# SwiGLU's activation turned by transposing transfers in place of TensorE

## The chip, the cores and the metric

The kernel runs on one core of one Trainium2 chip. The metric is device time of one execution in microseconds (us). Engines are named as in the profile: PE is TensorE's matmul side and PEld its weight loads, DVE is VectorE, ACT is ScalarE, POOL is GpSimd, SP is SyncE, which issues most DMA transfers. Each engine works through its own list of instructions in order.

## The reference

One layer of a decoder on 256 tokens of width 2048, in float32: an attention branch and a recurrent branch are merged, then comes the feed-forward network, then a gated embedding. The change lies in the feed-forward network alone:

```python
h = rms_norm(x, g_ffn_pre[layer])
gate, up = jnp.split(h @ w_gate_up[layer], 2, axis=-1)
x = x + rms_norm((jax.nn.silu(gate) * up) @ w_down[layer], g_ffn_post[layer])
```

`w_gate_up` is 2048 x 11264 and `w_down` is 5632 x 2048.

## The kernel before

**Tiles.** P is 128 and NB is 512. The 256 tokens are two chunks c of 128. The hidden width of 5632 is 11 blocks j of 512 columns (NJ). A product is made in three matmuls: every float32 operand is split into a rounded high part and the rest (`hi`/`lo` for activations, `wh`/`wl` for weights), and hi·wh, lo·wh and hi·wl are summed in a PSUM bank (`terms`, L473). Some groups of four weight tiles (quads) are done with seven products instead of eight (`by_quads`, L520).

**Preparing weights.** SP loads a pair of 128 x 512 weight tiles (`raw`, 512 KB) into one of six buffers; ACT makes `wh`, DVE makes `wl`, and for the quads DVE also makes sums `t` that ACT and DVE split in turn (`parts_of_pair`, L342; `parts_of_quad`, L364). Up to 61 general slots of 128 x 512 words (`slot`, L236) and seven `wh`/`wl` buffers hold what PE has not used yet.

**What sets the order.** The program is written by generators. A planner's clock advances with each matmul (0.227 us for a wide one, L40). A side task is a generator that yields what it waits for: an engine (its planned end), a tile, or a number of microseconds; `pump` (L219) continues those that are due. So side work is put among the matmuls at build time, and each engine then works in that fixed order.

**SwiGLU.** For block j, PE makes the gate and up products for both chunks. At the block's end DVE sums the partial results (`total`, L585), ACT applies Silu to the gate (`ev_g`, L1624), DVE multiplies (`ev_u`, L1638). The result t, 128 tokens x 512 columns, must be turned so that `w_down`'s products find the hidden width on the partitions. `gated` (L1609) does this: `transpose4` (L656) waits until three of the eight PSUM banks are free (`misc`, L270), has PE transpose four 128 x 128 squares against an identity into one bank, ACT copies the bank to `actT`, SP stores `actT` to a DRAM tile `actd[c][j]`. That is 22 tiles, two per block, and 88 transposes. From block 10 on POOL loads them back as `act` (`act_parts`, L1671) for the down product.

Because `misc` asks for three free banks, the transposes of most blocks stand one block late in the order: those of block 1 come when block 2's sums have been taken out.

Of the kernel before, what the change touches and what calls it, by code (L numbers as in the profile page):

```python
# [13 lines left out]
F32 = mybir.dt.float32  # L14
F32R = mybir.dt.float32r
I32 = mybir.dt.int32
AF = mybir.ActivationFunctionType
ALU = mybir.AluOpType
AX = mybir.AxisListType

P = 128
D = 2048
NB = 512
# [6 lines left out]

TABLES = (AF.Sigmoid, AF.Silu, AF.Exp, AF.Ln, AF.Sin)
TABLE_LOAD = 1.3
# [96 lines left out]
def block_kernel(ctx: ExitStack, tc: tile.TileContext, I, out: bass.AP):  # L129
# [24 lines left out]
    class InOrder:  # L154
# [20 lines left out]
        def __getattr__(self, name):  # L175
            f = getattr(self.engine, name)

            def call(o, *a, **kw):
                if name != "dma_start":
                    self.estimate(name, o, a, kw)  # L180
                return tc.keep_in_program_order(f(o, *a, **kw))  # L181

            return call

    V = InOrder(nc.vector, 0.07, 0.00105)
    A = InOrder(nc.scalar, 0.16, 0.0008)
    G, T, S = InOrder(nc.gpsimd, 0.9, 0.002), InOrder(nc.tensor, 0.0, 0.0), InOrder(nc.sync, 0.0, 0.0)
# [9 lines left out]
    def transpose(o, i, idn):  # L197
        clock[0] += SMALL
        T.transpose(o, i, idn)
# [29 lines left out]
    def nm(s):  # L229
        count[0] += 1  # L230
        return f"{s}_{count[0]}"
# [4 lines left out]
    def slot(s, shape=(P, NB), dt=F32):  # L236
        i = free_slots.popleft()
        t = slots.tile(list(shape), dt, tag=f"s{i}", name=nm(s))
        owner[id(t)] = i, t
        return t  # L240

    def free(*tiles):
        for t in tiles:
            free_slots.append(owner.pop(id(t))[0])
# [18 lines left out]
    def drop(ps):  # L263
        banks.append(bank_of.pop(id(ps))[0])
# [5 lines left out]
    def misc():  # L270
        while len(banks) < 3:
            yield 0.3
        return bank("misc")

    def act(o, i, f, **kw):
        return A.activation(o, i, f, **kw)

    def tt(o, a, b, op):
        return V.tensor_tensor(o, a, b, op)
# [12 lines left out]
    def cols(h, d=P):  # L292
        return slice(h * d, (h + 1) * d)
# [21 lines left out]
    def split_pair():  # L315
# [3 lines left out]
        if isinstance(raw, list):  # L319
            parts = [(slot("wh", dt=F32R), slot("wl", dt=F32R)) for j in range(2)]  # L320
            for (hi, lo), r in zip(parts, raw):
                act(hi, r, AF.Copy)
                tt(lo, r, hi.bitcast(F32), ALU.subtract)
            done = partial(free, *parts[0], *parts[1])
            free(*raw)
        elif len(in_pool) < SPLIT + 1:
            hi = wsplit.tile([P, 2, NB], F32R, tag="wh", name=nm("wh"))
            lo = wsplit.tile([P, 2, NB], F32R, tag="wl", name=nm("wl"))
            act(hi, raw, AF.Copy)
            tt(lo, raw, hi.bitcast(F32), ALU.subtract)  # L330
            parts, done = [(hi[:, j, :], lo[:, j, :]) for j in range(2)], in_pool.popleft
            in_pool.append(k)
        else:
            parts = [(slot("wh", dt=F32R), slot("wl", dt=F32R)) for j in range(2)]
            for j in range(2):
                act(parts[j][0], raw[:, j, :], AF.Copy)
            for j in range(2):
# [4 lines left out]
    def parts_of_pair():  # L342

        w, k, col, raw, _ = loaded.popleft()
        if len(in_pool) <= SPLIT:
            hi = wsplit.tile([P, 2, NB], F32R, tag="wh", name=nm("wh"))
            lo = wsplit.tile([P, 2, NB], F32R, tag="wl", name=nm("wl"))
            in_pool.append(k)
            act(hi, raw, AF.Copy)
            yield  # L350
            tt(lo, raw, hi.bitcast(F32), ALU.subtract)
            parts, done = [(hi[:, j, :], lo[:, j, :]) for j in range(2)], in_pool.popleft
        else:
            parts = [(slot("wh", dt=F32R), slot("wl", dt=F32R)) for j in range(2)]
            for j in range(2):
                act(parts[j][0], raw[:, j, :], AF.Copy)
            yield
# [271 lines left out]
    def lookup(groups):  # L629
        def there(g):  # L630
            return g in groups if isinstance(groups, dict) else len(groups) > g and groups[g] is not None

        def f(k):
            hurry(lambda: there(k // 4))
            hi, lo = groups[k // 4]
            return hi[:, k % 4, :], lo[:, k % 4, :]
        f.groups = groups
        return f
# [17 lines left out]
    def transpose4(src):  # L656
        ps = yield from misc()
        for i in range(4):
            transpose(ps[:, cols(i)], src[:, cols(i)], ident)
        return ps  # L660
# [146 lines left out]
    sinks = amask[:, 256:272]  # L807
    posi = cst.tile([P, 2], I32, name="posi")

# [223 lines left out]
    def hgrn_core(c, g):  # L1033
# [55 lines left out]
        def scores(lev):  # L1089
# [22 lines left out]
            if lev < 5:  # L1112
                V.copy_predicated(
                    right(sc),
                    cmask[:, cols(lev, 64)].rearrange("p (n w) -> p n w", w=w).unsqueeze(1)
                    .broadcast_to([P, 4, nb, w]).bitcast(I32),
                    pv.rearrange("p h (n w) -> p h n w", w=w))
# [488 lines left out]
    stored, parts, sides, down_sides = [set(), set()], [], {}, {}  # L1606
    h2T = [lookup(n.groups) for n in norm2]

    def gated(c, j, t):  # L1609

        pa = yield from transpose4(t)
        free(t)
        yield T
        at = slot("actT")
        act(at, pa, AF.Copy)
        drop(pa)
        S.dma_start(actd[c][j], at)
        free(at)
        stored[c].add(j)

    def swiglu(j):
# [16 lines left out]
        def ev_u(c, ps):  # L1638
            def f():
                if j in BY_QUADS and SEVEN:  # L1640
                    t = yield from total(us, 1, c, ps)
                    while sg[c] is None:
                        yield 0.3
                    yield sg[c]
                    stt(t, t, norm2[c].r, sg[c], ALU.mult, ALU.mult)
                    free(sg[c])
                else:
                    while sg[c] is None:
                        yield 0.3
                    t = sg[c]  # L1650
                    stt(t, ps, norm2[c].r, t, ALU.mult, ALU.mult)
                    drop(ps)
                yield V
                yield from gated(c, j, t)
            chain(f())
# [199 lines left out]
```

## Time and profile before

| | |
|---|---|
| Times of three runs | 1487.32, 1487.96 (median), 1491.14 us |
| The profiled execution's own time | 1489.56 us |
| Its span, first to last instruction | 1487.5 us |
| Mean granted TensorE clock | 0.997 |
| Gate and up products of blocks 0 to 10 | about 690 to 1155 us of the span |
| HBM read, written | 298.08 MB, 15.21 MB |

Busy time is a union over an engine's instructions. PE's matmuls overlap: one lasts 0.39 us, and the next one starts 0.227 us after it. What a group of PE instructions costs is therefore read from starts in the timeline and not from durations. DVE's and ACT's instructions overlap by some 0.1 us.

### The profile page before, as it was taken

To read this page: it belongs to the slowest core of one execution; us is meant where nothing else is said; L and a number is where in the kernel's file an instruction comes from. 1 tells how busy PE (TensorE), PEld (TensorE's weight loads), DVE (VectorE), ACT (ScalarE), POOL (GpSimd) and SP (SyncE) were. 2 spreads that over 40 slices of the span, in tenths; PEclk is the share of its full clock that TensorE was granted. 3 is DMA by queue.
4 is the path that set the end of the run, shared out by engine and by line. 5 is a ranking of instruction groups with operands and counts; after the bars stand their busy time and mean duration, and the time that the engine had idled before them with its cause. 6 is when DMAs were issued, how large, how long until landed. Compare 5 with 4: busy or idle time off the path is not lost.

```text
span 1487.5 us, 19958 instructions
## 1 busy us (share of the span) xinstructions
PE 1469.5 (99%) x6838; PEld 1216.3 (82%) x6838; DVE 1239.9 (83%) x2043; ACT 888.9 (60%) x1417; POOL 62.9 (4%) x107
## 2 busy tenths in 40 slices
PE   9999999999999999999999999999999999999997
PEld 6888888888887888888888888888888887888885
DVE  6878958755999867977899999999988899997773
ACT  7755655566666645665655666565655666575661
POOL 2100000000000100000000000000000000010000
PEclk9999999999999999999999999999999999999998
DMA  9754544345576856866756676576677678797551
GB/s 342 257 188 155 171 141 128 114 128 170 184 240 227 309 185 201 272 227 199 252 182 219 205 238 213 174 230 206 215 239 268 214 252 270 214 336 260 192 188 56
DMA packets 159557, 314.59 MB, mean 211 GB/s; under 512 B 11072, under 2 KB 11520, under 8 KB 159456
## 3 DMA queue, kind: packets, MB, share of 16 engines
q1 hardware_dynamic: 153024, 293.38, 61.0%
q0 software_dynamic: 6256, 19.88, 3.7%
q8 instruction: 53, 0.87, 0.2%
q14 instruction: 48, 0.39, 0.1%
q10 hardware_dynamic: 176, 0.07, 0.0%
HBM read 298.08 MB, written 15.21 MB: 211 GB/s over the span
## 4 chain that ended last, share of the span: by engine, by line
PE 64%; DVE 4%; issue 2%; DMA 1%; ACT 1%; DVEq 0%; POOLq 0%; POOL 0%; ACTq 0%
PE acc L181 63%; DVE wl L181 2%; PE misc L181 1%; DVE u L181 1%; ACT wh L181 1%; DVE t L181 1%; DMA raw<-in_w_in 1%; DMA raw<-in_w_down 0%; DMA raw<-in_w_gate_up 0%; DVE eg L181 0%; DVE slo L181 0%; DVE lo L181 0%; ACT hi L181 0%; DVE sides L181 0%; DVE s L181 0%
## 5 line engine op out<-in xcount | busy, mean ns | idle before, releaser
L181 PE MATMUL acc<-wh,hi 128*128 128x512 f32 x1769 | 700.2, 396 | 3.6 <-DVE u L181 2.4
L181 DVE TENSOR_TENSOR wl<-raw,wh 128x1024 fp32r<-128x1024 f32 (+1 forms) x606 | 595.7, 1007 | 115.4 <-ACT wh L181 113.8
L181 PE MATMUL acc<-wl,hi 128*128 128x512 f32 x1769 | 690.0, 390 | 0.0
L181 PE MATMUL acc<-wh,lo 128*128 128x512 f32 x1769 | 688.9, 389 | 0.0
L181 ACT ACTIVATE wh<-raw 128x1024 fp32r<-128x1024 f32 (+1 forms) x606 | 514.3, 883 | 239.8 <-PE acc L181 101.6
L181 PEld LDWEIGHTS acc<-wl,hi 128*128 128x128 f32 x1769 | 332.0, 188 | 71.2 <-DVE wl L181 1.1
L181 PEld LDWEIGHTS acc<-wh,hi 128*128 128x128 f32 x1769 | 332.3, 188 | 70.6 <-DVE u L181 3.2
L181 PEld LDWEIGHTS acc<-wh,lo 128*128 128x128 f32 x1769 | 332.5, 188 | 66.6 <-issue 0.2
L181 ACT ACTIVATE wh<-t 128x512 fp32r<-128x512 f32 x236 | 145.6, 628 | 106.6 <-DVE t L181 85.9
L181 DVE TENSOR_TENSOR wl<-t,wh 128x512 fp32r<-128x512 f32 x236 | 152.2, 683 | 0.5 <-PE acc L181 0.5
L181 DVE TENSOR_TENSOR u<-acc,u 128x512 f32<-128x512 f32 x132 | 86.3, 684 | 18.8 <-PE acc L181 17.6
L181 PE MATMUL acc<-wh,shi 128*128 128x512 f32 x236 | 91.9, 390 | 1.2 <-ACT shi L181 1.2
L181 PE MATMUL acc<-wh,slo 128*128 128x512 f32 x236 | 91.9, 390 | 0.2 <-DVE slo L181 0.2
L181 PE MATMUL acc<-wl,shi 128*128 128x512 f32 x236 | 91.8, 389 | 0.0
L181 DVE TENSOR_TENSOR t<-raw,t 128x512 f32<-128x512 f32 x118 | 81.1, 687 | 3.7
L181 PEld LDWEIGHTS acc<-wh,shi 128*128 128x128 f32 x236 | 44.3, 188 | 10.8 <-ACT shi L181 1.6
L181 PEld LDWEIGHTS acc<-wh,slo 128*128 128x128 f32 x236 | 44.3, 188 | 9.7 <-DVE slo L181 0.5
L181 PEld LDWEIGHTS acc<-wl,shi 128*128 128x128 f32 x236 | 44.3, 188 | 9.2
L181 POOL DMA_DIRECT2D act<-actd x40 | 21.4, 538 | 601.9 <-DVE wl L181 402.4
L181 DVE TENSOR_TENSOR t<-raw,raw 128x512 f32<-128x512 f32 x59 | 40.3, 684 | 3.9 <-DMA raw<-in_w_gate_up 1.9
L181 DVE TENSOR_TENSOR t<-raw 128x512 f32<-128x512 f32 x59 | 40.3, 684 | 0.0
L181 DVE TENSOR_TENSOR lo<-act,hi 128x512 fp32r<-128x512 f32 x40 | 27.2, 684 | 8.1 <-ACT hi L181 8.0
(214 smaller groups left out, 852.1 us busy)
## 6 DMA issues: line engine op xcount, KB each, us to landing
raw<-in_w_gate_up SPq DMA_DIRECT2D x176, 512.0 KB, 4.6
raw<-in_w_in SPq DMA_DIRECT2D x152, 512.0 KB, 4.3
raw<-in_w_down SPq DMA_DIRECT2D x88, 512.0 KB, 5.5
raw<-in_w_out SPq DMA_DIRECT2D x32, 512.0 KB, 5.5
raw<-in_w_ple_gate SPq DMA_DIRECT2D x32, 512.0 KB, 5.1
act<-actd POOLq DMA_DIRECT2D x40, 256.0 KB, 5.6
raw<-in_w_attn_branch SPq DMA_DIRECT2D x16, 512.0 KB, 5.2
raw<-in_w_hgrn_branch SPq DMA_DIRECT2D x16, 512.0 KB, 5.1
```

Of the source, the lines that this page charges most:

```text
L181: return tc.keep_in_program_order(f(o, *a, **kw))
```

## The change

`gated` no longer uses PE or PSUM. ACT separates the low and high 16-bit halves of t's words into two planes (`apart`, 128 x 1024 halfwords). A transposing DMA transfer, issued from ACT's queue, turns the eight 128 x 128 squares of halfwords from SBUF to SBUF (`turned`). The generator waits 7 us of the planner's clock. ACT then puts the halves together again (`actT`), and SP stores `actT` as before.

```diff
+U16 = mybir.dt.uint16
...
-                if name != "dma_start":
+                if not name.startswith("dma_start"):
...
+    def halves(t):
+        return t.bitcast(U16).rearrange("p (n two) -> p two n", two=2)
+
     def gated(c, j, t):
 
-        pa = yield from transpose4(t)
+        apart = slot("apart", (P, 2 * NB), U16)
+        act(apart.rearrange("p (two n) -> p two n", two=2), halves(t), AF.Copy)
         free(t)
-        yield T
+        turned = slot("turned", (P, 8, P), U16)
+        A.dma_start_transpose(turned, apart)
+        free(apart)
+        yield 7.0
         at = slot("actT")
-        act(at, pa, AF.Copy)
-        drop(pa)
+        act(halves(at), turned.rearrange("p (two c) t -> p two (c t)", two=2), AF.Copy)
+        free(turned)
+        yield A
         S.dma_start(actd[c][j], at)
         free(at)
         stored[c].add(j)
```

The added import shifts the helper's line, which all recorded instructions carry, from L181 to L182. The four places below are all of block 1's tiles.

PE, where the transposes of block 1 stood, among the matmuls that end block 2's up product (`acc` are PSUM sums, `misc` the bank of the transposes); rows of before:

```order
L181 MATMUL acc_7731<-wh_7580,lo_6508 128x512
L181 MATMUL acc_7731<-wl_7581,hi_6507 128x512
L181 MATMUL misc_7758<-ident,u_7290 128x128 x4
L181 MATMUL misc_7763<-ident,u_7292 128x128 x4
L181 MATMUL acc_7734<-wh_7589,hi_6377 128x512
```

The same place of the change:

```order
L182 MATMUL acc_7743<-wh_7592,lo_6508 128x512
L182 MATMUL acc_7743<-wl_7593,hi_6507 128x512
L182 MATMUL acc_7746<-wh_7598,hi_6377 128x512
L182 MATMUL acc_7746<-wh_7598,lo_6378 128x512
L182 MATMUL acc_7746<-wl_7599,hi_6377 128x512
```

The two groups of four are gone, and the matmuls on both sides meet. On PE nothing else differs in the whole program: it loses these 22 rows of four.

ACT at the end of block 1, after the two Silu (`u<-u,rest`); rows of before:

```order
L181 ACTIVATE u_7289<-u_7289,rest_6592 128x512
L181 ACTIVATE wh_7377<-t_7318 128x512
L181 ACTIVATE wh_7401<-raw_7259 128x1024
L181 ACTIVATE wh_7410<-raw_7272 128x512
L181 ACTIVATE wh_7412<-raw_7272 128x512
L181 ACTIVATE wh_7420<-raw_7383 128x512
L181 ACTIVATE wh_7422<-raw_7383 128x512
```

The same place of the change:

```order
L182 ACTIVATE u_7287<-u_7287,rest_6592 128x512
L182 ACTIVATE wh_7375<-t_7316 128x512
L182 ACTIVATE apart_7391<-u_7288 128x1024
L182 DMA_TRANSPOSE turned_7393<-apart_7391 128x8x128
L182 ACTIVATE wh_7403<-raw_7257 128x1024
L182 ACTIVATE apart_7406<-u_7290 128x1024
L182 DMA_TRANSPOSE turned_7408<-apart_7406 128x8x128
L182 ACTIVATE wh_7416<-raw_7270 128x512
```

ACT separates and issues right behind block 1's Silu, a block earlier than PE's transposes stood. Between the second issue and the copies that need its result stand eight splits of weights:

```order
L182 ACTIVATE wh_7454<-t_7452 128x512
L182 ACTIVATE wh_7468<-raw_7314 128x512
L182 ACTIVATE actT_7473<-turned_7393 128x2x512
L182 ACTIVATE actT_7481<-turned_7408 128x2x512
L182 ACTIVATE wh_7489<-t_7466 128x512
```

SP, at the stores of the same tiles; rows of before:

```order
L181 DMA raw_7716<-in_w_gate_up 128x2x512
L181 DMA raw_7746<-in_w_gate_up 128x2x512
L181 DMA actd_6434<-actT_7768 128x512
L181 DMA actd_6423<-actT_7774 128x512
L181 DMA raw_7813<-in_w_gate_up 128x2x512
```

And of the change:

```order
L182 DMA raw_7464<-in_w_gate_up 128x2x512
L182 DMA raw_7495<-in_w_gate_up 128x2x512
L182 DMA actd_6434<-actT_7473 128x512
L182 DMA actd_6423<-actT_7481 128x512
L182 DMA raw_7542<-in_w_gate_up 128x2x512
```

The stores stand twelve weight loads earlier; weight loads stand behind them in both.

## The prediction

> **What bounds the kernel now.** I read the page's busy times first, then the table by stretches for the part that the change touches, then the waits there.
>
> ```profile
> PE 1469.5 (99%) x6838; PEld 1216.3 (82%) x6838; DVE 1239.9 (83%) x2043; ACT 888.9 (60%) x1417; POOL 62.9 (4%) x107
> ```
>
> ```profile
> core 0: us, PE busy (x) PEld busy (x) DVE busy (x) ACT busy (x) POOL busy (x), PEclk, DMA share, GB/s
> 740.00:1165.00 425.00, 424.54 (x1909) 351.00 (x1908) 397.86 (x568) 256.02 (x382) 5.38 (x10) 1.00 0.67 214
> ```
>
> 740 to 1165 us holds ten of the eleven pairs of turned tiles. PE works without a hole there, at full granted clock. DVE is close behind: of 425 us it has only 425 − 397.86 = 27.1 us idle. ACT has 169 us idle. So PE is the bound and DVE the next one. The waits of the same stretch:
>
> ```profile
> PEld misc L181 <- DVE u L181: 2.1, 6, 0.8
> DVE u L181 <- PE acc L181: 8.1, 4, 2.2
> DVE wl L181 <- ACT wh L181: 5.4, 7, 1.5
> ACT wh L181 <- DMA raw<-in_w_gate_up: 50.6, 28, 4.0
> ACT wh L181 <- DVE t L181: 41.5, 46, 4.6
> ACT actT L181 <- PE misc L181: 34.9, 10, 5.9
> ACT wh L181 <- PE acc L181: 24.5, 14, 2.7
> ```
>
> PE's products wait for nobody; the only waits on its side belong to the transposes that go. The preparing engines wait for PE to release buffers. How far they are ahead shows when the order of DVE and of PE is laid beside their times. The first of these three `wl` ends at 877.75; PE first reads it at 888.55:
>
> ```profile
> 877.07 1.89 DVE L181 TENSOR_TENSOR wl<-t,wh 128x512 fp32r<-128x512 f32 x3
> ...
> 888.55 0.39 PE L181 MATMUL acc<-wl,shi 128*128 128x512 f32 x1
> ```
>
> That is a lead of 10.8 us, about the smallest that I find between 740 and 1120 us (the median is 15); one of 8.4 follows at 1128.
>
> **What is removed.** 88 transposes, of which 80 in that stretch:
>
> ```profile
> L181 PE MATMUL misc<-ident,u 128*128 128x128 f32 x80 | 11.1, 277 | 0.5 <-DVE u L181 0.4
> ```
>
> The mean of 277 ns isn't their price, since PE's instructions overlap. I read it from starts, at block 1's pair, the dearest and the last:
>
> ```profile
> 814.28 0.39 PE L181 MATMUL acc<-wh,lo 128*128 128x512 f32 x1
> 814.51 0.39 PE L181 MATMUL acc<-wl,hi 128*128 128x512 f32 x1
> 814.74 1.13 PE L181 MATMUL misc<-ident,u 128*128 128x128 f32 x8
> 815.62 0.49 PE L181 MATMUL acc<-wh,hi 128*128 128x512 f32 x1
> 815.95 0.40 PE L181 MATMUL acc<-wh,lo 128*128 128x512 f32 x1
> ...
> 898.75 0.39 PE L181 MATMUL acc<-wl,hi 128*128 128x512 f32 x1
> 899.55 1.25 PE L181 MATMUL misc<-ident,u 128*128 128x128 f32 x8 [0.42 <-DVE u L181]
> 900.56 0.48 PE L181 MATMUL acc<-wh,hi 128*128 128x512 f32 x1
> 900.88 0.40 PE L181 MATMUL acc<-wh,lo 128*128 128x512 f32 x1
> ...
> 1157.54 0.39 PE L181 MATMUL acc<-wl,hi 128*128 128x512 f32 x1
> 1157.77 1.03 PE L181 MATMUL misc<-ident,u 128*128 128x128 f32 x8
> 1158.56 0.48 PE L181 MATMUL acc<-wh,hi 128*128 128x512 f32 x1
> 1158.87 0.40 PE L181 MATMUL acc<-wh,lo 128*128 128x512 f32 x1
> ```
>
> Normally starts follow each other by 0.227 us (814.28 to 814.51). From the last product before the pair to the second one after it 1.44 us pass, where two steps are 0.45: the pair costs 0.98 us. At 899 it costs 2.13 − 0.45 = 1.68, with a wait in it; at 1157 it costs 0.88. The eleven pairs, read alike, sum to **11.3 us** (10.4 in the stretch). It stands whole on the path that sets the end, because PE has no hole that it could fall into.
>
> The Trainium skill speaks of another price: "TensorE: Matmul & The Clock Gate", Part 4: PE-mode transpose, gives about 275 ns for one in a kernel's context. By that figure 88 would be an estimated 24.2 us and the kernel would come to 1463.8. The trace shows the same 277 ns as a duration, yet only about 0.11 us of lost starts for each, so the measurement decides against that sum.
>
> **What is added, on ACT.** For each tile:
>
> ```profile
> L181 ACT ACTIVATE wh<-raw 128x1024 fp32r<-128x1024 f32 x92 | 94.4, 1052 | 56.2 <-DMA raw<-in_w_gate_up 34.6 <-PE acc L181 17.2 <-ACT wh L181 2.9
> L181 ACT ACTIVATE actT<-misc 128x512 f32<-128x512 f32 x20 | 11.5, 597 | 34.9 <-PE misc L181 34.9
> 1.21 0.49 ACTq L181 DMA_DIRECT2D grow<-in_g_mix_pre  x1
> ```
>
> `apart` and the new `actT` handle 1024 elements each. No row shows halfwords at a stride: the ends are 0.60 us (the same bytes as words) and 2.1 (twice the row of 1024); I take 1.05, the row with the same count. Issuing the transposing transfer isn't shown either. The ends are 0.49, ACT's own issue of a plain transfer, and 2.4, the landing of a store of the same 256 KB (quoted below), if ACT had to stay with it to the end; I take 0.49, the row of the same engine. So a tile costs ACT 2 × 1.05 + 0.49 − 0.60 = 2.0 us and all 22 cost 44 us, against 169 idle ones. In sum this is hidden; it matters only where ACT is late for DVE. The place, after block 1's Silu in before:
>
> ```profile
> 774.58 0.62 ACT L181 ACTIVATE wh<-t 128x512 fp32r<-128x512 f32 x1
> 775.10 3.36 ACT L181 ACTIVATE wh<-raw 128x1024 fp32r<-128x1024 f32 x5
> 781.48 0.63 ACT L181 ACTIVATE wh<-t 128x512 fp32r<-128x512 f32 x1 [3.02 <-DVE t L181]
> 782.63 0.63 ACT L181 ACTIVATE wh<-t 128x512 fp32r<-128x512 f32 x1 [0.51 <-DVE t L181]
> 783.41 0.63 ACT L181 ACTIVATE wh<-t 128x512 fp32r<-128x512 f32 x1 [0.15 <-DVE t L181]
> 783.95 0.62 ACT L181 ACTIVATE wh<-raw 128x512 fp32r<-128x512 f32 x1
> 784.62 0.63 ACT L181 ACTIVATE wh<-t 128x512 fp32r<-128x512 f32 x1
> ```
>
> Two `apart` and two issues, 3.1 us, now go in between 774.58 and 776. Behind them stand the weight splits that DVE wants next. But 3.02 us of idle time follow at 781.48, so ACT is level again there. I put DVE's wait at 0 to 1 us for a pair.
>
> What may DVE wait? Once PE runs 10.4 us faster, DVE's idle time in the stretch is 27.1 − 10.4 = 16.7 us, and its lead of 10.8 can be used up as well: 27.5 us over ten pairs, **2.7 us a pair**, cost PE nothing. Beyond that each microsecond a pair costs ten in all. With 0 to 1 us a pair I cost ACT's part at nothing; if the idle time after it were gone, the full 3.1 us a pair would cost (3.1 − 2.7) × 10 = 4 us.
>
> **The wait that is added.** `actT` now waits for a landing, and the splits of the next weights queue behind it on ACT, then DVE, which waits for those. Between issue and `actT` stands what ran from 775.10 to 784.62 in before, 9.5 us. Landings of 256 KB, first the store of `actT` and then a reload in the mixer:
>
> ```profile
> DMA to landing us min/median/max: 2.0/2.4/5.7
> ...
> DMA to landing us min/median/max: 2.3/7.1/9.3
> ```
>
> All lie below 9.5, the first at 2.4 by far, so I cost the wait at nothing. The ends are no hold at all and, with two transfers of a pair in line at 9.3 each, 18.6 − 9.5 = 9.1 us of hold a pair. Block 0's pair has only two splits between issue and use and may hold ACT a few microseconds once; the lead covers that.
>
> **The stores on SP** move with it: 22, as many as before, with the weight loads queued behind them as before. Should the store wait for ACT, loads come later by as much; that falls under the hold above. The transfers add 22 × 0.26 MB = 5.8 MB to some 91 MB of the stretch (214 GB/s × 425 us), 6% of traffic at a DMA share of 0.67. PSUM is relieved: turning a tile takes no bank.
>
> **The sum.** −11.3 us on PE, the rest hidden. Of the profiled execution's 1489.56 us that leaves 1478.3 (its span 1487.5, with 2.06 around it). It ran 1.6 us above the median of 1487.96, so against the median I get 1476.7; I say **1477.0**.
>
> **Rivals.**
>
> *DVE or ACT becomes the bound in part.* For: DVE has only 16.7 us to spare, and halfwords or the issue may be dearer than my rows. Against: the lead, and ACT's 169 us. If 3.1 us a pair reach DVE, 4 us of the gain go: 1476.7 + 4 = about 1480.7.
>
> *The gain is eaten.* The issue takes 2.4 us instead of 0.49: two `apart` and two issues are 6.9 us a pair; less the 3.02 of idle time behind them 3.9 reach DVE; (3.9 − 2.7) × 10 = 12 us are lost: 1476.7 + 12 = 1488.7, no change. For: a transfer that reorders may need many pieces to be issued. Against: nothing in this trace.
>
> *Slower: the landings hold ACT.* Each microsecond past 9.5 from issue to landing holds ACT, DVE and, past 2.7 a pair, PE. It decides from 2.7 + 1.13 = 3.8 us of hold a pair, a landing at 13.3 us. Two transfers in line at the reload's median of 7.1 make 14.2, a hold of 4.7: (4.7 − 2.7) × 10 = 20 us, 1476.7 + 20 = 1496.7. At 18.6 it would be 64 us. For: both transfers of a pair go out on one queue into engines that are 67% busy. Against: the store of the same size lands in 2.4 us on the same engines.
>
> The Trainium skill has a rule for this rival: "VectorE: DVE Perf Modes", The three transpose paths, gives 1309 ns for one 128 x 128 square by the DMA crossbar, against 390 on TensorE, and its rules prefer TensorE where PSUM will do. Eight squares one after another would be an estimated 10.5 us and a pair 21, which is this rival's case. "Advanced Engine Details and Errata", X-Bar Transpose (TRN2), says the opposite, 350 to 400 GB/s, an estimated 0.7 us for a tile. No row here shows either.
>
> **How the numbers follow.** What a measurement of this kernel can tell from no change is about 0.3%, 4.5 us. Forecast (1475.5 to 1479): 0.56. Partly eaten (to 1485): 0.15, of which 0.12 still count as faster. Eaten: 0.10. Slower: 0.19, half of it below 1494. Faster 0.56 + 0.12 = 0.68; same 0.03 + 0.10 = 0.13; slower 0.19. The range from 1475.5 to 1494 leaves out the far half of the slower case and a little below. The forecast alone would stand at 1475.5 to 1479.
>
> **What would show it.** Right: PE's starts run through at 0.227 us where the pairs stood; DVE's idle time in the stretch shrinks to about 17 us; ACT's waits before `actT` for `turned` are absent or under 1 us. Wrong: long transposing issues on ACT's queue; waits of ACT for `turned` of some microseconds, with DVE waiting for `wh` behind them; waits of PE for `wl`; or weight loads that land later than before.

## The result, and the profile after

| | before | after |
|---|---|---|
| Median of seven runs | 1487.96 us | 1493.71 us |
| Lowest to highest | 1487.32 to 1491.14 | 1488.82 to 1497.82 |
| The profiled execution's own time, its span | 1489.56, 1487.5 | 1497.82, 1495.6 |

The ratio is 1.0032, with a 95% interval of 1.0017 to 1.0047: the change makes the kernel slower by about 5 us (5.75 between the medians), where 11 us less were forecast. The profiled execution after is the slowest of its seven, 4.1 us above the median, which matters below.

Busy times of the page, and the same stretch as before in the table by stretches (PE, PEld, DVE, ACT, POOL busy, clock, DMA share, GB/s):

```profile
PE 1468.0 (98%) x6750; PEld 1209.8 (81%) x6750; DVE 1242.5 (83%) x2043; ACT 921.2 (62%) x1439; POOL 62.9 (4%) x107
```

```profile
740.00:1165.00 425.00, 416.76 (x1820) 340.08 (x1819) 399.68 (x572) 283.08 (x399) 5.38 (x10) 1.00 0.76 227
```

PE was almost without a hole here before (0.5 us); now 8.2 of 425 us are idle. DVE still has 25.3 us idle, not 17. So PE is held, and not by an engine that has run out of time. The waits of the stretch (engine, what it made, what it waited for: us in total, times, longest):

```profile
ACT u L182 <- DVE u L182: 38.8, 9, 4.6
ACT wh L182 <- DMA raw<-in_w_gate_up: 35.7, 20, 4.1
...
PEld acc L182 <- DVE u L182: 14.8, 16, 1.3
DVE wl L182 <- ACT wh L182: 13.3, 19, 0.9
...
PE acc L182 <- DVE u L182: 8.2, 14, 0.9
ACT wh L182 <- DMA turned<-apart: 5.3, 3, 1.9
```

Four things are to be read here. DVE waits for ACT's weight splits 13.3 us instead of 5.4. PE's products and their weight loads wait for DVE's `u`; in the profile before only the transposes had such a wait (0.4 and 2.1 us). DVE's own wait for PE at `u` (8.1 us before) is gone: at `u` DVE used to be first, now it is late. And ACT hardly stands for the transfers: 5.3 us in three waits.

Where that happens shows in the timeline at the end of a block. `u<-acc,u` empties PSUM banks; a block takes four banks for its products and four for its quads' sums, all eight, so the next block's first products need the banks that `u` gives back. After, at the end of block 3:

```profile
856.89 0.39 PE L182 MATMUL acc<-wl,hi 128*128 128x512 f32 x1
857.20 1.41 DVE L182 TENSOR_TENSOR u<-acc,u 128x512 f32<-128x512 f32 x2
...
857.95 0.50 PE L182 MATMUL acc<-wh,hi 128*128 128x512 f32 x1 [0.67 <-DVE u L182]
...
858.53 0.68 DVE L182 TENSOR_TENSOR wl<-raw,wh 128x512 fp32r<-128x512 f32 x1
...
859.13 0.69 DVE L182 TENSOR_TENSOR t<-raw 128x512 f32<-128x512 f32 x1
859.23 0.39 PE L182 MATMUL acc<-wl,hi 128*128 128x512 f32 x1
859.73 4.00 DVE L182 TENSOR_TENSOR u<-acc,u 128x512 f32<-128x512 f32 x6
860.47 0.50 PE L182 MATMUL acc<-wh,hi 128*128 128x512 f32 x1 [0.86 <-DVE u L182]
```

and before, at the same place:

```profile
854.73 2.48 DVE L181 TENSOR_TENSOR u<-acc,u 128x512 f32<-128x512 f32 x4 [2.17 <-PE acc L181]
```

Before, DVE stood 2.17 us and waited for PE. After, DVE begins `u` only at 857.20, when PE has started the last product for which it has a bank (856.89); PE stands there and again at 860.47. Such holes stand at seven of the block boundaries; the delays of PE's starts in them sum to 12.4 us.

**The whole account.** The table gives the lag of the same matmul behind the profile before (negative is ahead; the transposes of `u` and `sg` are left out of the count, which are the 88 of the turned tiles and 8 that all these kernels have):

| matmul number | 3000 | 3600 | 4200 | 4800 | 5400 | 6000 | 6600 |
|---|---|---|---|---|---|---|---|
| time in before, us | 621.6 | 755.1 | 893.1 | 1034.0 | 1173.8 | 1311.9 | 1444.5 |
| after | +1.86 | +0.94 | +3.03 | +4.90 | +3.08 | +8.10 | +8.11 |
| e1, transposes taken out alone | −0.15 | −1.06 | −3.02 | −7.89 | −11.78 | −12.38 | −12.37 |
| e4, plain transfer instead | −0.36 | −1.29 | −2.75 | −6.05 | −9.19 | −10.05 | −10.03 |
| e13, issue on SP, two copies more | −0.36 | −1.32 | +3.07 | +6.81 | +8.13 | +13.03 | +13.04 |
| e15, issue on SP, buffer kept | +0.07 | −0.89 | −2.85 | −7.62 | −11.51 | −9.73 | −9.72 |

After loses 1.9 us before the change's first instruction, in an idle time of PE at 469 us and the slower matmuls behind it, which vary from execution to execution. Over the feed-forward products, 3000 to 5400, it loses 1.2 us, where −11.3 were expected. Then two holes in the down product cost 5.0 us together; the timeline of PE there, and the row of the table by stretches for the second:

```profile
1221.27 0.50 PE L182 MATMUL acc<-wh,lo 128*128 128x512 f32 x1 [0.63 <-DVE lo L182]
...
1242.07 0.39 PE L182 MATMUL acc<-wl,hi 128*128 128x512 f32 x1
1245.04 0.79 PE L182 MATMUL acc<-wh,shi 128*128 128x512 f32 x1 [2.58 <-ACT shi L182]
```

```profile
1242.00:1252.00 10.00, 7.41 (x20) 5.19 (x19) 8.06 (x16) 7.93 (x12) 0.00 (x0) 0.66 0.44 128
```

The first costs 1.0 us; before has no wait there. The idle time of 2.58 us (1.22 at this place before) is followed by some 6 us at a granted clock below 1 (0.66 as the mean of these 10 us): 1.4 us are lost in the one and 2.6 in the other. The first share is no work of the change: in the profiles of all these kernels, which are alike up to there, that idle time at 469 us lies between 1.34 and 1.99 us, and behind some of them the clock drops. The third is taken up at the end. The question for the experiments is the middle: what takes 12.5 us of the feed-forward part.

### The profile page after: what moved, and what is told of

Same layout as the page of the kernel before. It is cut to its first block, busy times and chain, and to the rows that moved or that the text cites. A ratio compares the mean times of both kernels' runs of the same rounds, so it can differ in the third digit from the quotient of the medians.

```text
span 1495.6 us, 19832 instructions
## 1 busy us (share of the span) xinstructions
PE 1468.0 (98%) x6750; PEld 1209.8 (81%) x6750; DVE 1242.5 (83%) x2043; ACT 921.2 (62%) x1439; POOL 62.9 (4%) x107
## 4 chain that ended last, share of the span: by engine, by line
PE 55%; DVE 10%; issue 3%; DMA 3%; ACT 2%; ACTq 0%; DVEq 0%; SPq 0%; POOLq 0%; POOL 0%
PE acc L182 54%; DVE wl L182 5%; DVE u L182 2%; DVE t L182 2%; ACT wh L182 2%; DMA raw<-in_w_gate_up 1%; PE misc L182 1%; DMA raw<-in_w_in 1%; DMA raw<-in_w_down 1%; ACTq L182 0%; ACT apart L182 0%; DVE eg L182 0%; ACT actT L182 0%; DVE lo L182 0%; DVE slo L182 0%
## 5 line engine op out<-in xcount | busy, mean ns | idle before, releaser
L182 PE MATMUL acc<-wh,hi 128*128 128x512 f32 x1769 | 701.5, 397 | 11.5 <-DVE u L182 11.2
L182 DVE TENSOR_TENSOR wl<-raw,wh 128x1024 fp32r<-128x1024 f32 (+1 forms) x606 | 596.9, 1009 | 128.2 <-ACT wh L182 126.4
L182 PE MATMUL acc<-wl,hi 128*128 128x512 f32 x1769 | 690.6, 390 | 0.0
L182 PE MATMUL acc<-wh,lo 128*128 128x512 f32 x1769 | 689.5, 390 | 0.6 <-DVE lo L182 0.6
L182 ACT ACTIVATE wh<-raw 128x1024 fp32r<-128x1024 f32 (+1 forms) x606 | 512.9, 882 | 229.8 <-PE acc L182 114.0
L182 PEld LDWEIGHTS acc<-wh,hi 128*128 128x128 f32 x1769 | 332.4, 188 | 85.2 <-DVE u L182 18.6
L182 PEld LDWEIGHTS acc<-wl,hi 128*128 128x128 f32 x1769 | 332.3, 188 | 71.5 <-DVE wl L182 1.3
L182 PEld LDWEIGHTS acc<-wh,lo 128*128 128x128 f32 x1769 | 332.8, 188 | 67.2 <-DVE lo L182 1.1
L182 ACT ACTIVATE wh<-t 128x512 fp32r<-128x512 f32 x236 | 143.0, 625 | 91.1 <-DVE t L182 74.6
L182 DVE TENSOR_TENSOR wl<-t,wh 128x512 fp32r<-128x512 f32 x236 | 152.5, 685 | 3.4 <-ACT wh L182 1.6
L182 PE MATMUL acc<-wh,shi 128*128 128x512 f32 x236 | 93.4, 396 | 2.6 <-ACT shi L182 2.6
L182 DVE TENSOR_TENSOR u<-acc,u 128x512 f32<-128x512 f32 x132 | 86.9, 686 | 10.8 <-PE acc L182 8.7
L182 PE MATMUL acc<-wh,slo 128*128 128x512 f32 x236 | 93.2, 395 | 0.0
L182 PE MATMUL acc<-wl,shi 128*128 128x512 f32 x236 | 92.8, 393 | 0.0
L182 DVE TENSOR_TENSOR t<-raw,t 128x512 f32<-128x512 f32 x118 | 81.2, 688 | 3.7
L182 PEld LDWEIGHTS acc<-wh,shi 128*128 128x128 f32 x236 | 45.1, 191 | 12.4 <-ACT shi L182 3.0
L182 PEld LDWEIGHTS acc<-wh,slo 128*128 128x128 f32 x236 | 45.1, 191 | 10.0 <-DVE slo L182 0.5
L182 PEld LDWEIGHTS acc<-wl,shi 128*128 128x128 f32 x236 | 45.2, 191 | 9.5
L182 POOL DMA_DIRECT2D act<-actd x40 | 21.4, 538 | 608.1 <-DMA raw<-in_w_gate_up 393.6
L182 DVE TENSOR_TENSOR t<-raw,raw 128x512 f32<-128x512 f32 x59 | 40.4, 685 | 3.8 <-DMA raw<-in_w_down 1.9
L182 DVE TENSOR_TENSOR t<-raw 128x512 f32<-128x512 f32 x59 | 40.4, 684 | 0.0
L182 ACT ACTIVATE u<-u,rest 128x512 f32<-128x512 f32 x20 | 13.8, 716 | 38.8 <-DVE u L182 38.8
```

## The experiments

Theories. **T1, cover**: the transposes stood where PE must wait for the banks anyway. **T2**, later **I** and **L**: ACT's added time makes DVE late at `u`; I puts it on the transposing issue, L on any load beyond a budget. **T3**, later **D**: the transfers slow the weight loads. **T4**, later **O**: the planner's new order is at fault. **H** and **W**: ACT stands for the landings. **Q**: issuing from ACT's queue is bad in itself, whatever its time. Where a kernel leaves the turning out, its expectation says so.

### e1_no_pe: the transposes taken out, nothing put in

```diff
-        pa = yield from transpose4(t)
-        free(t)
+        pa = yield from misc()
         yield T
         at = slot("actT")
-        act(at, pa, AF.Copy)
+        act(at, t, AF.Copy)
+        free(t)
```

> The kernel before, without its 88 transposes on TensorE; the PSUM bank is still taken and given back, ACT copies the tile itself (128x512, about 0.6 us) and the store stays at its place. It leaves out the turning of the 22 tiles. Theory T1 (cover: the transposes stood where PE must wait for DVE to empty PSUM banks for the next block anyway, so taking them away frees little): the gain in the FFN is 0 to 3 us, a time of 1485 to 1488 beside 1488 of before, and PE shows new waits for DVE's u at the block boundaries. Theory T2 (ACT's added 3.06 us a tile makes DVE late, and that alone eats the gain): nothing is added here, so the 11.3 us are won in the FFN, about 1476.7, or up to 1482 if the later down phase gives back 5.

Measured: 1478.03 (1477.09 to 1478.69) beside 1488.83 of before; ratio 0.9930 (0.9917 to 0.9943). The stretch:

```profile
740.00:1165.00 425.00, 425.00 (x1876) 351.91 (x1875) 407.12 (x588) 264.25 (x395) 7.52 (x14) 1.00 0.70 221
```

PE has no hole. T1 falls: 11.6 us are won in the feed-forward part (−0.15 to −11.78 in the table), and this is the floor for what the change could give.

### e2_light: the early place, without PE and without a transfer

```diff
-        apart = slot("apart", (P, 2 * NB), U16)
...
-        yield 7.0
+        yield from room(1)
         at = slot("actT")
-        act(halves(at), turned.rearrange("p (two c) t -> p two (c t)", two=2), AF.Copy)
-        free(turned)
+        act(at, t, AF.Copy)
+        free(t)
```

> The changed kernel's early place for the activation, without PE's transposes and without a transfer: one copy of 0.6 us on ACT and the store. It leaves out the turning of the 22 tiles. ACT has as little work as before, 3.06 us a tile less than in the changed kernel. T2: about 1477 to 1482. T1 (cover): 1485 to 1489, with PE waiting for u at the block boundaries as in the changed kernel. T4 (the hole at 1242 us with the slower pitch behind it comes from the shifted order of the down phase): whatever the FFN gains, the 5 us there are lost or not by the order alone.

Measured: 1479.33 (1477.53 to 1481.62); ratio 0.9940 (0.9928 to 0.9952). The early place costs next to nothing by itself (1.3 us more than e1, and the same 11.6 us won in the feed-forward part). The idle time of the down product is here too, 1.24 us as in before, without a drop of the clock behind it. That speaks against T4, though DVE's order in e2 is not that of after. T4 falls with e3 and e4 below: they have DVE's and SP's order of after to the row, lose only 2.2 and 2.8 us against e1 in the feed-forward part, and nothing in the down product.

### e3_no_transfer and e4_plain: no transfer, and a plain one

```diff
         free(t)
-        turned = slot("turned", (P, 8, P), U16)
-        A.dma_start_transpose(turned, apart)
-        free(apart)
         yield 7.0
         at = slot("actT")
-        act(halves(at), turned.rearrange("p (two c) t -> p two (c t)", two=2), AF.Copy)
-        free(turned)
+        act(halves(at), apart.rearrange("p (two n) -> p two n", two=2), AF.Copy)
+        free(apart)
```

> The changed kernel without the 22 transposing transfers and their issues on ACT's queue: apart stays, and actT is copied straight from it. It leaves out the turning of the 22 tiles. The orders of PE, DVE and SP are those of the changed kernel. T2 (ACT's load): ACT loses 1.25 us of issue and some 0.3 us of a dearer actT for each tile, 3.1 us a pair, so DVE's waits for wh fall from 13.3 us towards 5.4 and PE's bank waits shrink: some 4 to 8 us below the changed kernel's 1493.7. T1 (cover) and T4 (the order of DVE's u): no change, 1492 to 1494. T3 (the transfers slow the weight loads): as T2, but then with DMA's share falling from 0.76 to about 0.67 and loads landing earlier.

```diff
-        A.dma_start_transpose(turned, apart)
+        A.dma_start(turned, apart.rearrange("p (c t) -> p c t", c=8))
```

> The changed kernel with a plain transfer of the same 256 KB on the same queue of ACT in place of the transposing one. It leaves out the turning of the 22 tiles. T3 (transposing transfers are the trouble, by their issue of 1.25 us or by the DMA time they take): the issue falls to about 0.5 us and DMA's share towards 0.70, and the time to 1488 or below. T2: a gain of some 2 us only (1.5 us of ACT a pair). T1 and T4: within 1 us of the changed kernel.

Measured: e3 1482.44 (1481.11 to 1483.49), ratio 0.9959 (0.9947 to 0.9971); e4 1482.12 (1479.63 to 1486.36), ratio 0.9964 (0.9950 to 0.9977). The two copies on ACT cost some 4 us against e1, a plain transfer of the same 256 KB nothing more, and the transposing one 11.6 us more. These steps are larger than T2 had given them (4 to 8 us for e3, 2 for e4), and e4's time is what T3 had said, which named two reasons in one, the issue and the time of the DMA engines. From here on they are held apart, as I and D. What differs, first the rows of `turned` in e4 (count, then least, median and greatest duration in ns), then in after:

```profile
L182 ACTq DMA_DIRECT2D turned<-apart x22: 472/472/509, 732.2 to 1152.7; - x22
...
DMA to landing us min/median/max: 2.3/4.7/5.3
```

```profile
L182 ACTq DMA_TRANSPOSE turned<-apart x22: 1247/1249/1920, 734.4 to 1166.2; - x22
L182 ACT ACTIVATE actT<-turned x22: 1347/1361/1382, 739.3 to 1176.7; 128x1024 uint16<-128x1024 uint16 x22
...
DMA to landing us min/median/max: 2.7/5.2/10.5
```

The landing is hardly longer in the median; the issue holds ACT 1.25 us instead of 0.47. DMA's share is 0.74 in e4 and 0.76 in after, so T3 has little room.

### e7_three and e12_two: long issues without transposing

```diff
-        A.dma_start_transpose(turned, apart)
+        flat = apart.rearrange("p (c t) -> p c t", c=8)
+        A.dma_start(turned[:, 0:3], flat[:, 0:3])
+        A.dma_start(turned[:, 3:6], flat[:, 3:6])
+        A.dma_start(turned[:, 6:8], flat[:, 6:8])
```

> The changed kernel with three plain transfers (of 3, 3 and 2 eighths of the tile) on ACT's queue in place of the one transposing transfer: ACT issues for about 3 x 0.47 = 1.41 us, a little more than the transposing issue's 1.25, and the DMA engines see only plain pieces. It leaves out the turning of the 22 tiles. Theory I (the transposing transfer's longer issue on ACT makes DVE late for the PSUM banks at the next block's start): close to the changed kernel, 1490 to 1495. Theory H (its landing holds ACT) and theory D (its small pieces slow the weight loads): as with one plain transfer, 1481 to 1484.

e12_two does the same with two halves:

> The changed kernel with two plain transfers of half a tile on ACT's queue in place of the transposing one: about 1.0 to 1.2 us of issue a tile. It leaves out the turning of the 22 tiles. Theory I gives a time on the line through 0.47 us (1482.1), 1.28 (1493.7) and 1.74 (1501.6): 1488 to 1493. If three transfers were dear for another reason (their number, or descriptors of a smaller size): 1482 to 1485.

Measured: e7 1501.57 (1501.11 to 1503.06), ratio 1.0090 (1.0076 to 1.0104), with 1.74 us of issue a tile, more than I had reckoned; e12 1487.78 (1485.01 to 1491.58), ratio 0.9996 (0.9986 to 1.0006), with 1.10 us. e7 lies above the range that I gave it, e12 just below. Plain pieces do harm too, and the more, the longer their issues hold ACT. D, in the form that it takes a transposing transfer, falls as the main cause.

### e8_later_use and e14_keep: the landings

e8 replaces `yield 7.0` by `yield 14.0`.

> The changed kernel with the use of the turned tile planned 14 instead of 7 us behind the issue. Theory H (the 6 us that ACT stands waiting for the landing, and DVE behind it): these waits go and with them the loss, 1482 to 1486. Theories I and D: within 2 us of the changed kernel, 1491 to 1495; in between if hold and issue share it.

Measured: 1495.46 (1493.96 to 1496.85); ratio 1.0046 (1.0033 to 1.0058). ACT no longer waits for `turned` at all, DVE for 2.7 us, and the time is no better. H falls for this order; e6 below is the stronger sign against it.

e14 moves `free(apart)` behind `actT`. In after, a weight split takes over apart's buffer at once and so waits until the transfer has read it; these are the 5.3 us of `wh` waiting for `turned`.

> The changed kernel, in which the buffer of apart is given back only after actT, not at the issue; everything is computed. In the changed kernel a weight split that takes over the buffer at once waits for the transfer to land: 5.3 us of ACT's waits in the FFN. Theory W (these waits are part of the loss): they go, and 2 to 5 us with them, 1489 to 1492. If they are covered: 1493 to 1494.5.

Measured: 1497.43 (1495.95 to 1498.87); ratio 1.0064 (1.0052 to 1.0077). The waits of `wh` go, the time rises beyond both ranges. W falls too, for this order.

### e5_late and e9_told: another place, and a planner that knows

e5 waits for three free banks ahead of `apart`, as the transposes had done:

```diff
+        while len(banks) < 3:
+            yield 0.3
         apart = slot("apart", (P, 2 * NB), U16)
```

> The changed kernel with apart and the transposing transfer put where the transposes on TensorE stood, some microseconds later in the next block. Everything is computed. Theories I, H and D see the same work at another place: 1490 to 1495. If the place matters (behind the first weight splits of the new block ACT is ahead of DVE again and the issue falls into ACT's idle time), 1481 to 1487.

Measured: 1493.58 (1492.84 to 1497.13); ratio 1.0040 (1.0028 to 1.0053), as after. It is better in the feed-forward part (−1.8 to −5.2 of lag between matmuls 3600 and 5400) and gives it back in the down product, where PE stands longer for the last tiles' `lo`.

e9 adds the issue to the planner's estimate:

```diff
+        A.until = max(clock[0], A.until) + 1.25
         A.dma_start_transpose(turned, apart)
```

> The changed kernel, with 1.25 us added to the planner's estimate of ACT at each transposing issue, which it had taken to be free; everything is computed. Theory O (the planner's order is at fault, because it doesn't know of the issue's time: steps that wait for ACT come due too early and DVE's work is queued in a bad order): 1481 to 1487. Theory I (it is ACT's load; the order can't take it away): 1490 to 1495.

Measured: 1509.29 (1505.79 to 1514.85); ratio 1.0139 (1.0120 to 1.0158). A miss on both sides: the order moves (some 270 rows of difference on DVE), ACT now stands 19.2 us in six waits before `actT`, the longest 9.5, and DVE 40.8 behind its splits. O is not the cure in this form; why the new order is so bad was not followed up.

### e6_sp: the issue on SP

```diff
-        A.dma_start_transpose(turned, apart)
+        yield A
+        S.dma_start_transpose(turned, apart)
```

> The changed kernel with the transposing transfer issued from SP's queue, by a step of the planner that follows apart. Everything is computed. Theory I: ACT loses 1.25 us a tile, and the time is that of the kernel without a transfer, 1481 to 1484, if SP, which issues the weight loads too, stands the 1.25 us. Theory H: the landing stays and comes later still, 1490 to 1495. Theory D: about 1493.

Measured: 1481.92 (1480.31 to 1485.21); ratio 0.9956 (0.9942 to 0.9969). The issue takes as long there, with one of 3.4 us, but SP has the time:

```profile
L182 SPq DMA_TRANSPOSE turned<-apart x22: 1242/1251/3389, 735.9 to 1157.3; - x22
```

```profile
740.00:1165.00 425.00, 425.00 (x1876) 351.91 (x1876) 407.32 (x587) 294.43 (x412) 5.38 (x10) 1.00 0.78 234
```

PE is without a hole, with a larger DMA share than after has (0.78) and the same median landing (5.2 us). ACT and DVE even wait longer for the landings than in after, 11.4 us in this stretch:

```profile
ACT wh L182 <- DMA turned<-apart: 5.6, 2, 4.2
...
DVE t L182 <- DMA turned<-apart: 3.5, 1, 3.5
...
DVE wl L182 <- DMA turned<-apart: 1.2, 1, 1.2
ACT actT L182 <- DMA turned<-apart: 1.1, 2, 0.8
```

That takes the last support from D and H. It leaves I, L and Q.

### e10_dummy, e13_dummy2, e16_plain_dummy: a load on ACT that is no issue

e10 and e13 add to e6 one and two copies that only repeat `apart`, not told to the planner; e16 adds one to e4.

```diff
         act(apart.rearrange("p (two n) -> p two n", two=2), halves(t), AF.Copy)
+        tc.keep_in_program_order(nc.scalar.activation(
+            apart.rearrange("p (two n) -> p two n", two=2), halves(t), AF.Copy))
```

> The kernel with the transposing transfer on SP's queue, with ACT's copy into apart made twice (1.04 us more of ACT's time for each tile, not told to the planner, so that every order stays; everything is computed). Theory I as a load on ACT, whatever it is made of: between the points measured so far (0.47 us of issue a tile on ACT gave 1482.1, 1.28 gave 1493.7) 1.04 us stands for about 1490; 1488 to 1493. If it is something about issuing from ACT's queue itself rather than ACT's time: as the kernel with the issue on SP, 1481 to 1484.

Measured: 1481.07 (1480.11 to 1486.05); ratio 0.9955 (0.9941 to 0.9968). Theory I in the form "every microsecond on ACT costs the same" fails: 1 us a tile more leaves the whole time where it was. It is not free, though. In the profiled executions e6 wins 11.7 us in the feed-forward part (matmuls 3000 to 5400) and e10 only 8.0; the down product, where e6 loses 3.8 against before and e10 wins 1.1, hides that. Either the load has a budget, if a soft one (L), or issues are special (Q).

> The kernel with the issue on SP's queue and two more copies into apart on ACT for each tile (about 1.9 us of ACT's time, each copy starting 0.95 us behind the one before). Everything is computed. Theory L (ACT's load with a budget: about 1 us a tile on top of apart and actT is free, beyond that each us a tile costs some 15 to 22 us): 1493 to 1502. Theory Q (it is issuing transfers from ACT's queue that costs, not ACT's time): 1481 to 1484, as with one copy more.

> The kernel with one plain transfer on ACT's queue (0.47 us of issue, 1482.1), with the copy into apart made twice. All orders are the changed kernel's; it leaves out the turning of the 22 tiles. Beyond apart and actT ACT now has 0.47 us of issue, some 0.25 us in which it runs dry round the issue, and 0.95 us of copy, 1.67 us, against some 1.5 us in the changed kernel. Theory L: 1490 to 1497, though nothing is transposed. Theory Q: within 2 us of 1482.1.

Measured: e13 1504.48 (1502.16 to 1506.80), ratio 1.0115 (1.0100 to 1.0130); e16 1498.07 (1494.12 to 1503.33), ratio 1.0071 (1.0055 to 1.0087). Both a little above L's ranges, far from Q's. In e13 ACT issues nothing, and the same waits come back:

```profile
PEld acc L182 <- DVE u L182: 21.8, 21, 1.6
DVE wl L182 <- ACT wh L182: 17.9, 17, 2.3
...
PE acc L182 <- DVE u L182: 12.9, 20, 1.2
```

Q falls. The dose can be read from starts: how long a tile keeps ACT from the start of `apart` until its next instruction. In e10 that is 907.48 − 905.44 = 2.04 us, in after 912.89 − 910.53 = 2.36:

```profile
905.44 1.04 ACT L182 ACTIVATE apart<-u 128x1024 uint16<-128x1024 uint16 x1
906.51 1.06 ACT L1618 ACTIVATE apart<-u 128x1024 uint16<-128x1024 uint16 x1
907.48 0.62 ACT L182 ACTIVATE wh<-t 128x512 fp32r<-128x512 f32 x1
```

```profile
910.53 1.04 ACT L182 ACTIVATE apart<-u 128x1024 uint16<-128x1024 uint16 x1
911.60 1.25 ACTq L182 DMA_TRANSPOSE turned<-apart  x1
912.89 0.63 ACT L182 ACTIVATE wh<-t 128x512 fp32r<-128x512 f32 x1 [1.32 <-DVE wl L182]
```

Medians over the tiles (the next start taken as 0.05 us behind an issue or 0.09 ahead of a copy's end, as such rows show), beside the times:

| kernel | e3, e6 | e4 | e10 | e12 | after | e16 | e7 | e13 |
|---|---|---|---|---|---|---|---|---|
| ACT per tile, us | 0.95 | 1.59 | 2.04 | 2.25 | 2.37 | 2.69 | 2.90 | 3.14 |
| time, us | 1482.4, 1481.9 | 1482.1 | 1481.1 | 1487.8 | 1493.7 | 1498.1 | 1501.6 | 1504.5 |
| lost against e1 between matmuls 3000 and 5400, us | 2.2, 0.0 | 2.8 | 3.7 | 5.9 | 12.8 | 17.2 | 19.3 | 20.1 |

The last row is taken from one profiled execution of each and leaves out what happens ahead of the feed-forward part and behind it. There the loss rises with ACT's time at every step, whatever that time is made of, but not evenly. Up to about 2 us a tile it is small, and the whole time doesn't show it; beyond, it is steep. From e10 to e13, 1.10 us on each of 22 tiles, 24.2 us of ACT's time, cost 23.4 us at the end, of which 16.5 show in the feed-forward part and 6.0 in the down product. From e12 to after 0.12 us a tile, 2.6 us in all, go with 7.0 us in the feed-forward part: more than ACT's time alone explains.

### e11_pool: the first copy on POOL

In e6, `G.tensor_copy` makes `apart` in place of ACT.

> The kernel with the transposing transfer on SP's queue, with the copy into apart moved from ACT to POOL, which is nearly idle; everything is computed. It relieves ACT by another 1.04 us a tile. If ACT's load still costs something at that point: 1477 to 1481. If not, the same as with apart on ACT, 1481 to 1484. If POOL's copy takes many microseconds or slows DVE while it runs: 1485 or more.

Measured: 1494.95 (1492.96 to 1496.59); ratio 1.0040 (1.0028 to 1.0052). This is the branch in which POOL's copy slows DVE. POOL's copy, DVE's split beside it, and DVE's next one:

```profile
908.96 1.44 POOL L182 COPY apart<-u 128x1024 uint16<-128x1024 uint16 x1 [1.27 <-DVE u L182]
```

```profile
909.42 1.52 DVE L182 TENSOR_TENSOR wl<-raw,wh 128x512 fp32r<-128x512 f32 x1
910.87 0.68 DVE L182 TENSOR_TENSOR wl<-t,wh 128x512 fp32r<-128x512 f32 x1
```

The DVE instruction takes 1.52 us instead of 0.68 and ends 0.5 us after the copy does. The Trainium skill, "SBUF — State Buffer", SBUF: two separate sides, says that a DVE operation with two SBUF inputs and a GpSimd operation that reads SBUF lock each other out for a whole instruction; these rows agree. Counted over the stretch, where DVE's `wl` of `raw`, `t` of one `raw` and `lo` are longer in the mean than in e6, the difference is an estimated 15 us of DVE's time.

### e15_sp_keep: both cures

e6 with `free(apart)` behind `actT`.

> The kernel with the issue on SP's queue, with apart's buffer kept as well; everything is computed. Theory L leaves little to win here, since the load is already within the budget: 1479 to 1483, against 1481.9. If it comes below 1480 it is the best of the versions that compute everything.

Measured: 1479.99 (1477.91 to 1481.11) beside 1487.75 of before; ratio 0.9945 (0.9933 to 0.9957). It is faster than before by 0.55% and within 2 us of the floor of e1; in the feed-forward part it wins 11.6 us, as e1 does. Whether keeping the buffer adds to e6 can't be said: the intervals of the two ratios overlap.

## Why the prediction was wrong, step by step

**The bound.** PE was the bound and gave what was said once nothing else was added: e1. That "what DVE may wait" could be read from DVE's idle time and the lead of `wl` was wrong in its place. The place is PSUM: no lead spans a block boundary there, because a block's eight banks leave none for the next one. "PSUM is relieved" was true of the misc bank and missed this; DVE's idle time did not fall to 17 us, and PE never waited for `wl`.

**What is removed: 11.3 us.** Right; e1 won 11.6 in this part, 10.8 in the median (0.13 us for each transpose, where the prediction has 0.11). The Trainium skill's 275 ns for a transpose ("TensorE: Matmul & The Clock Gate", Part 4), taken as a price and so an estimated 24.2 us, is refuted by the same run.

**What is added, on ACT: 2.0 us a tile, at no cost.** This is the step that failed: the term was too small, and it was put at nothing. `apart` was right: 1.04 against 1.05. The issue was taken at 0.49 from a plain transfer's row; it is 1.25, between the two bounds that were given. `actT` was taken at 1.05 and is 1.36. So a tile adds 1.04 + 1.25 + 1.36 − 0.60 = 3.05 us. A shorter issue alone would not have saved the forecast: with e4, where it is 0.47 as supposed, the kernel comes to 1482.1, and without any issue (e3) to 1482.4. That is close to the rival in which ACT costs a part (1480.7).

**The price of exceeding it.** 3.02 us of ACT's idle time and 2.7 us a pair were to be free, 5.7 together, and only `apart` and the issue, 3.1 us, were set against them. This rule failed as well. With the measured rows the same terms make 4.6 us a pair, 1.6 beyond the idle time, which by the rule still costs nothing. With the dearer `actT` (2 × 0.76) they make 6.1, 0.4 too much, which by the rule costs 4 us. The feed-forward part lost 12.8 against e1. The loss also begins below the limit: counted as the table counts, with `actT`, e4 has 2 × (1.59 + 0.76) = 4.7 us a pair and lost 2.8, e10 has 5.6 and lost 3.7. "Each microsecond a pair costs ten in all" fits beyond it as a size: from e10 to e13, 2.2 us a pair, it is 7.5 for each in the feed-forward part and 10.6 at the end; from e12 to e16, 0.88 a pair, 13 in the feed-forward part. What the step from e12 to after has beyond that stays open: the landings were tried (e8, e14) and did not bring it.

**The wait that is added: nothing.** Right in effect. Landings reached 10.5 us, more than the 9.3 taken, but without ACT's waits for them (e8) the time is the same, and with 11.4 us of waits for them (e6) PE has no hole. The rival in which they hold ACT, and with it the estimate of 10.5 us a tile from the Trainium skill's table of transpose paths ("VectorE: DVE Perf Modes"), did not come: the median is 5.2 for eight squares, and the greatest 10.5 is about that estimate.

**The rivals.** "The gain is eaten" named the right instruction and the right path, the issue's time on ACT that reaches DVE, and put the issue at 2.4 us with 1488.7. It is 1.25 us, and by that rival's own sum would have cost nothing; with the tighter limit, the dearer `actT` and the loss in the down product it came to 1493.7. It had been given one chance in ten, although the text itself found nothing in the trace against it. That 1493.7 lies just within the stated range is luck: the range reached up to 1494 for the landings' sake, which were not the cause.

**What stays open** is the down product, where 5.0 us of the profiled execution's loss lie. At the place of the idle time at 1245 us PE stands in most kernels: 0.3 us in e4, 0.6 in e1, 1.2 in before and e2, 1.3 in e15 and 2.6 in after, and the clock drops behind some of them (after, e15) and not behind others. The wait for `lo` some 20 us ahead of it is in after and in nine others, and not in before, e1 to e4, e10 and e15. It doesn't look like chance alone: from matmul 5400 on, the profiled execution of every changed kernel that came to 1487 us or more loses 2.5 to 9.0 us against before, while e1, e2, e3, e4 and e10 lie between −1.1 and +0.2. But e6 and e15 are fast and lose 3.8 and 1.8. No run was made to settle it.

## What to carry to other kernels

Price the issue of a DMA by its kind and shape, not by the next plain one in the trace, and put it on the queue of an engine that has time: moving this one from ACT to SP turned 0.3% slower into 0.4% faster. The Trainium skill, "DMA: Bandwidth & Descriptors", Issuing engines are not separate DMA queues, says that another issuing engine saves only the sequencer's time, "usually small relative to the DMA itself"; here that time was 1.25 us beside a landing of 5.2, and it was what decided. Where an engine's total has 30% to spare, look at the spot between two handovers: here the loss began below 5 us of ACT's time a pair of tiles, and beyond 5.6 us each further microsecond cost PE 0.75 us or more.

## What the runs showed of the hardware

- A transposing transfer of 128 x 1024 halfwords takes 1.25 us to issue, on ACT and on SP; a plain one of the same size 0.47. It lands in 2.7 to 10.5 us (median 5.2), the plain one in 2.3 to 5.3 (4.7).
- ACT's copy of 1024 halfwords takes 1.04 us when it reads at a stride of two (`apart`), 1.36 when it writes so (`actT`).
- Behind some of PE's idle times, from 1.29 us (e15) to 4.3 (e9), matmuls start 0.427 us apart instead of 0.227 for 5 to 12 starts; behind others, of 1.59 us (before) and 2.06 (e5), they don't. The length of the idle time alone does not decide it.
